# Expert lists of a retrieval layer: one-hot rows used one step later from three buffers, and 32 tiles of values for both token blocks in place of 33

## The chip, the cores and the metric

The kernel runs on one core of a Trainium2 chip. The metric is the device time of one execution in microseconds (us). Before the change three runs took 1665.8, 1665.89 and 1667.91 us, so the median is 1665.89 us.

## The reference, cut to what matters

256 tokens of width 2048 go through one layer: a pooling and an attention branch with an output projection, then a product-key retrieval over 16,384 experts, then a gated embedding. What the change touches is the retrieval:

```python
e1, e2 = ...                     # top 16 of 128 keys, 8 heads, two halves
eidx = e1 * 128 + e2             # 128 experts for each token
gates = softmax(vs)
def block(args):                 # 128 tokens at a time: two blocks
    xb, ib, gb = args
    act = gelu(einsum('tkd,td->tk', expert_u[ib], xb))
    return einsum('tk,tkd->td', act * gb, expert_v[ib])
```

So a row of `expert_v` matters only where `act * gb` is not zero for some token.

## The kernel before, in words

Every float32 product is made of three matmuls of split operands (`mm3`, lines 198 to 200): ScalarE casts a part of a raw tile to the high half (line 91), VectorE subtracts to get the low half (line 93).

After the front, the U stage computes the hidden units of all 128 x 128 experts, one row of 128 experts per step (`feat_mm`, `u_done`), times their gates, into coefficients [expert, token] that SyncE writes to DRAM (`write_coefs`). Free moments between the rows take side tasks: `used` (the largest coefficient of each expert in each block), and then in three stages (rows 0 to 95, 96 to 119, 120 to 127, `STAGES`) the making of lists. `classes` sorts the experts by the blocks that use them: both, the first alone, the second alone. `ranks` and `places` give each used expert a place in the list of its class. The lists have `CAPS` tiles of 128 places. An expert whose rank lies beyond its list is left over, and `places3` notes that in `over`.

`columns` (line 1026) then makes one-hot rows for four rows of experts at a time: `ol` (place within a tile, line 1040), `oh` (tile, line 1041, times the expert's number within its row, line 1042, and times the number of the row, line 1043). `into_list` (line 1048) multiplies them on TensorE, four matmuls per group (line 1053), and `list_end` and `indices` turn the sum into row numbers of V and of the coefficients. A place that no expert took gets row 0 of V and the row of zeros of the coefficients.

The V stage goes tile by tile over the lists (`v_tile`, line 1150): GpSimd gathers 128 rows of V (1 MB, `load_v`, line 1106) and the 128 rows of coefficients (`coef_load`, line 1119); ScalarE and VectorE split both; TensorE makes 24 matmuls of 128x512 for a tile of both blocks, 12 for a tile of one block. V's raw tiles lie in two pools in turn: tile numbers that are odd in `vraw` (three buffers), even ones from number 14 on in `raw` of the weight stream. The first 17 tiles (`EARLY`) are of the first block alone, and 11 of them run between the last rows of U; the others follow in an order that spreads the classes evenly (lines 167 to 175), and the last tile is always the last one for both blocks (`last_tile`). Six tiles before the end the stream takes two `raw` slots for weights (lines 1301 to 1303). From the first projection of the embeddings until tile 17, TensorE, VectorE and ScalarE run in the order of the code; everywhere else a planner orders them. GpSimd's and SyncE's queues run in the order in which their instructions stand.

The gate and the output end the kernel (`tail`, line 1306). Behind it stands a branch (line 1413): when `over` says that an expert found no place, `all_values` (line 1378) computes the sum again over all 128 tiles of V with a loop, one tile per turn, every tile with a single buffer, and the tail runs once more.

Of the kernel before, what the change touches and what calls it, by code (L numbers as in the profile page):

```python
# [19 lines left out]
P = 128  # L20
T = 256
# [8 lines left out]
# tiles of 128 experts that tokens of both blocks use, or of the first or the second block alone  # L30
CAPS = (33, 32, 32)
# [3 lines left out]
# the lists grow in stages, as the rows of 128 experts come; the first tiles of the first block alone  # L35
# start before the last stage
# [3 lines left out]
# of them, those between the last rows' hidden units, from this row on  # L40
BETWEEN = 11
START = 116
# parts of V that Pool splits, while the last lists are made
ON_POOL = (1, 2)
# columns of the lists, for pairs of bf16
# [5 lines left out]
class Feed:  # L51
    """The stream of weights: loads run ahead of the splits, splits ahead of the products."""
# [52 lines left out]
def emit(tc, a):  # L105
# [27 lines left out]
    # ---------------------------------------------------------------- the stream  # L133
# [34 lines left out]
    # tiles for both blocks and for one block in turn, so that loads and products keep pace  # L168
# [11 lines left out]
    # the last units wait for the values  # L180
# [15 lines left out]
    # ---------------------------------------------------------------- helpers  # L196
# [16 lines left out]
    def tok_mm(kts, n, lhs, psl, after=None, t_major=False):  # L213
        """psl[t][:, :n] = sum over kts of lhs[:, kt, t]^T @ W, parts of W from the stream."""
        lh, ll = lhs
        kts = list(kts)
        i = 0
        part = 0
        while i < len(kts):
            wh, wl, w = feed.get()  # L220
            k = w // n
            whv = wh.rearrange("p (k n) -> p k n", n=n)
            wlv = wl.rearrange("p (k n) -> p k n", n=n)
            order = [(j, t) for j in range(k) for t in range(2)]
            if t_major:
                order = [(j, t) for t in range(2) for j in range(k)]
            for j, t in order:
                kt = kts[i + j]
                ts = slice(t * P, (t + 1) * P)
                mm3(psl[t][:, :n], lh[:, kt, ts], ll[:, kt, ts], whv[:, j, :], wlv[:, j, :],  # L230
                    start=(i + j == 0), stop=(i + j == len(kts) - 1))
            i += k
            (after or hook)(*((part,) if after else ()))
            part += 1

    def feat_mm(bh, bl, ps, after):
        """ps[:, :T] = W^T @ (bh + bl), W [P, KT, 128] from the stream."""
        for i in range(2):
            wh, wl, _ = feed.get()
            whv = wh.rearrange("p (k n) -> p k n", n=P)  # L240
            wlv = wl.rearrange("p (k n) -> p k n", n=P)
            for j in range(8):
                kt = 8 * i + j
                mm3(ps[:, :T], whv[:, j, :], wlv[:, j, :], bh[:, kt, :], bl[:, kt, :],
                    start=(kt == 0), stop=(kt == KT - 1))
            if i == 0:
                after(0)

    # ---------------------------------------------------------------- front: loads and constants
# [6 lines left out]
    # the gains come with the first k-tile of x  # L256
# [55 lines left out]
    # ---------------------------------------------------------------- input projection, query latents  # L312
# [3 lines left out]
    def after_q(part):  # L316
        # part 0..3 are the k-tiles of the first unit, then two k-tiles each
        if part in (0, 4, 6):
            g = {0: 1, 4: 2, 6: 3}[part]
            if part == 0:  # L320
                xl[2] = load_x(2)
            split_x(g, xl[g])
            if part == 4:
                xl[3] = load_x(3)
# [3 lines left out]
    # small operands  # L328
# [18 lines left out]
    # latents: statistics and transposes (in the slots of y)  # L347
# [7 lines left out]
    # the latents stay unscaled by the norm of x: it goes into the scale of what follows them  # L355
# [13 lines left out]
    def lat_norm(i):  # L369
        # rstd1 * rsqrt(rstd1^2 * mean(z^2) + eps)  # L370
        for _ in range(2):
            dve.tensor_tensor(ssl[:, :, i], ssl[:, :, i], rstd1, op=OP.mult)
        rsqrt_mean(rl[:, :, i], ssl[:, :, i], 512, f1)
        dve.tensor_tensor(rl[:, :, i], rl[:, :, i], rstd1, op=OP.mult)
# [53 lines left out]
    # ---------------------------------------------------------------- queries, keys and values  # L428
# [88 lines left out]
    # ---------------------------------------------------------------- pool channels  # L517
# [28 lines left out]
    # ---------------------------------------------------------------- attention, pooling, output projection  # L546
# [11 lines left out]
    def scores(j):  # L558
        """two heads: keys of block 0 for the first queries, all keys for the second"""
# [92 lines left out]
    # ---------------------------------------------------------------- h and its norms  # L652
# [5 lines left out]
    # every value twice, side by side  # L658
# [73 lines left out]
    # ---------------------------------------------------------------- retrieval  # L732
# [55 lines left out]
    def slots_T(t):  # L788
        pt = bank()
        for i, s in enumerate((e12[t][:, 0], e12[t][:, 1], gate[t])):  # L790
            pe.transpose(pt[:, i * P:(i + 1) * P], s.rearrange("p h k -> p (h k)"), ident)
        ts = slice(t * P, (t + 1) * P)
        dve.tensor_copy(e1T[:, ts, :], pt[:, 0:P, None].to_broadcast([P, P, 2]))
        dve.tensor_copy(e2T[:, ts, :], pt[:, P:2 * P, None].to_broadcast([P, P, 2]))
        # the gates as a sum of three bf16 values, which is exact
        rest = sel.tile([P, P], F32, name="grest", tag="grest")
        part = sel.tile([P, P], BF16, name="gpart", tag="gpart")
        dve.tensor_copy(rest, pt[:, 2 * P:3 * P])
        for i in range(3):
            dve.tensor_copy(part, rest)  # L800
            if i < 2:
                dve.tensor_copy(gT[:, i, ts, :], part[:, :, None].to_broadcast([P, P, 2]))
                dve.tensor_tensor(rest, rest, part, op=OP.subtract)
            else:
                dve.tensor_copy(gT2[:, ts], part)
# [43 lines left out]
    # ---------------------------------------------------------------- hidden units and gates of all experts  # L849
# [32 lines left out]
    def group(g):  # L882
        """gates of four tokens, by expert; the first tiles hold activations already"""
# [26 lines left out]
    # coefficients to DRAM: a row of zeros, the first N0 rows of 128 experts, the others  # L910
# [16 lines left out]
    def used(lo, hi, b):  # L927
        """the largest coefficient of each expert in a block"""
# [12 lines left out]
    def open_vp():  # L941
# [3 lines left out]
        st["pr"] = vp.tile([P, 2 * T], F32, name="pr")  # L945
# [15 lines left out]
    def classes(s):  # L961
        """experts by the blocks that use them: both, the first alone, the second alone"""
# [18 lines left out]
    def ranks(s):  # L981
        """the place of each expert in the list of its class"""
# [7 lines left out]
    def places(s):  # L990
# [5 lines left out]
        for c in range(3):  # L996
# [3 lines left out]
            if c == 1 and s == len(STAGES) - 2:  # L1000
                dve.scalar_tensor_tensor(ok, r, EARLY * P - 0.5, ok, op0=OP.is_gt, op1=OP.mult)
# [17 lines left out]
    def places3(s):  # L1019
        # experts that found no place  # L1020
# [5 lines left out]
    def columns(s, k):  # L1026
        """the experts i1 = k to k + 3 of all i2: their places, and i1 + 1 and i2 there"""
        if s < 2:
            into_list(s)
# [9 lines left out]
        oh = st["vp"].tile([P, 2, 4, NL], BF16, name="oh", tag="oh", bufs=2)  # L1039
# [8 lines left out]
    def into_list(s):  # L1048
        out = st["list"][:, :2 * NL].rearrange("p (a n) -> p a n", a=2)
        while st["oh"]:  # L1050
# [13 lines left out]
    def indices(i):  # L1064
        """rows of V and of the coefficients; a free place takes any row of V and the zero coefficients"""
# [10 lines left out]
        # rows of half the tokens for the experts of one block  # L1076
# [61 lines left out]
    def last_tile(after):  # L1138
        """the values of the last tile, for both blocks, one after the other"""
# [10 lines left out]
    def v_tile(n, f, after=lambda i: None):  # L1150
        """the values of one tile of experts"""
# [28 lines left out]
    for j in range(NE):  # L1180
        ps = bank()
        if j == 0:
            # the scores of the last keys, then the front's memory is given back
# [22 lines left out]
        # the experts in use so far, from here on with all of their coefficients  # L1206
# [26 lines left out]
    # ---------------------------------------------------------------- per-layer embedding, first half  # L1233
    vp = st["vp"]
    pp = [vp.tile([P, D], F32, name=f"pp{t}") for t in range(2)]
# [4 lines left out]
    def proj(n, between=lambda: None):  # L1240
        """the embeddings' columns; what follows runs while the banks are read"""
# [36 lines left out]
    # ---------------------------------------------------------------- values  # L1278
# [26 lines left out]
    # ---------------------------------------------------------------- gate and output  # L1305
# [71 lines left out]
    # ---------------------------------------------------------------- lists that were too short  # L1377
    def all_values():
        """the sum over all experts, in their order, for inputs that use more than the lists hold"""
# [117 lines left out]
```

## Time and profile before

| what | value |
|---|---|
| median of three runs | 1665.89 us |
| the profiled execution (its span) | 1666.6 us |
| TensorE busy | 1641.0 us, 98% of the span, 11295 matmuls |
| VectorE busy | 1229.6 us, 74% |
| ScalarE busy | 914.9 us, 55% |
| GpSimd busy | 367.4 us, 22% |
| DMA traffic | 354.27 MB, mean 213 GB/s |

The page lists the profiled execution's time as its span, 0.7 us above the median. TensorE is busy nearly all of the time, so what another engine does counts only where TensorE waits for it. The few such waits are found in TensorE's timeline, where the number in brackets behind an instruction is the idle time before it and what ended it.

### The profile page before, as it was taken

Reading aid. Unit: us, or ns where it says so; the run is one execution under the profiler, and the core shown is the slowest. Engines: PE = TensorE matmul, PEld = TensorE weight load, DVE = VectorE, ACT = ScalarE, POOL = GpSimd, SP = SyncE. Lnnn points to the kernel's source line nnn. Section 1 sums busy time; section 2 is a strip of 40 time slices with the busy share of each in tenths; the row PEclk is TensorE's granted clock in tenths of the full one; section 3 lists DMA queues with packets and bytes.
Section 4 is the critical chain, followed back from the end, with each engine's and each line's share of the span. In section 5 each row is a group of like instructions: output and inputs, shape, how many; then the busy total and the mean of one; then the engine's idle time right before and its main releaser. Section 6 shows DMA issues by size and latency. Waiting matters only on the chain.

```text
span 1666.6 us, 29151 instructions
## 1 busy us (share of the span) xinstructions
PE 1641.0 (98%) x11295; PEld 1497.1 (90%) x11295; DVE 1229.6 (74%) x2299; ACT 914.9 (55%) x1598; POOL 367.4 (22%) x355
## 2 busy tenths in 40 slices
PE   8999999999999999999999999999989999999998
PEld 7888788999999999999999999999967888888886
DVE  6575667999986888998765558767786667667764
ACT  7765446544544777776444443345555566566653
POOL 0010000000000333333000000042256677766000
PEclk9999999999999999999999999999999999999999
DMA  8652356445555344444787554578678888888463
GB/s 304 224 194 101 128 201 223 159 176 178 179 182 181 142 151 151 136 151 148 259 277 277 205 203 166 189 291 282 224 271 316 287 298 295 282 298 290 153 219 111
DMA packets 55044, 354.27 MB, mean 213 GB/s; under 512 B 7633, under 2 KB 8786, under 8 KB 14578
## 3 DMA queue, kind: packets, MB, share of 16 engines
q1 hardware_dynamic: 35426, 239.08, 41.2%
q0 software_dynamic: 17600, 110.24, 18.6%
q10 hardware_dynamic: 1872, 3.02, 0.5%
q8 instruction: 90, 1.47, 0.3%
q14 instruction: 56, 0.46, 0.1%
HBM read 331.34 MB, written 20.97 MB: 211 GB/s over the span
## 4 chain that ended last, share of the span: by engine, by line
PE 95%; DVE 2%; DMA 1%; ACT 1%; issue 1%; DVEq 0%; ACTq 0%
PE bank L198 30%; PE bank L199 29%; PE bank L200 29%; PE bank L887 3%; DVE lo L93 1%; DMA raw<-in_w_in_q 1%; PE bank L1053 1%; ACT hi L91 1%; PE bank L815 0%; DMA raw<-in_V,idx 0%; PE bank L570 0%; PE bank L572 0%; PE bank L612 0%; PE bank L1329 0%; PE bank L693 0%
## 5 line engine op out<-in xcount | busy, mean ns | idle before, releaser
L93 DVE TENSOR_TENSOR lo<-raw,hi 128x1024 fp32r<-128x1024 f32 (+2 forms) x498 | 602.3, 1212 | 261.8 <-ACT hi L91 254.5
L91 ACT CAST hi<-raw 128x1024 fp32r<-128x1024 f32 (+2 forms) x498 | 513.9, 1033 | 494.9 <-PE bank L199 333.5
L198 PE MATMUL bank<-xnH,hi 128*128 128x256 f32 x2048 | 589.0, 288 | 0.4 <-issue 0.4
L200 PE MATMUL bank<-xnH,lo 128*128 128x256 f32 x2048 | 581.0, 284 | 0.8 <-DVE lo L93 0.8
L199 PE MATMUL bank<-xnL,hi 128*128 128x256 f32 x2048 | 580.9, 284 | 0.0
L198 PEld LDWEIGHTS bank<-xnH,hi 128*128 128x128 f32 x2048 | 391.9, 191 | 1.4 <-issue 0.6
L200 PEld LDWEIGHTS bank<-xnH,lo 128*128 128x128 f32 x2048 | 391.7, 191 | 1.3 <-DVE lo L93 1.0
L199 PEld LDWEIGHTS bank<-xnL,hi 128*128 128x128 f32 x2048 | 392.0, 191 | 0.4
L1119 POOL DMA_INDIRECT cr<-coefD,idx x97 | 129.3, 1333 | 372.3 <-ACT hi L91 295.0
L199 PE MATMUL bank<-lo,ccH 128*128 128x512 f32 x520 | 205.7, 396 | 1.3 <-issue 0.7
L200 PE MATMUL bank<-hi,ccL 128*128 128x512 f32 x520 | 205.1, 394 | 0.0
L876 POOL TENSOR_TENSOR oo<-m,gT 128x256 bf16<-128x256 bf16 x128 | 86.0, 672 | 423.6 <-DVE oo L874 252.4
L93 DVE TENSOR_TENSOR lo<-vraw,hi 128x1024 fp32r<-128x1024 f32 x108 | 131.4, 1224 | 53.8 <-ACT hi L91 50.7
L198 PE MATMUL bank<-hi,ccH 128*128 128x512 f32 x520 | 155.9, 397 | 2.0 <-ACT hi L91 2.0
L91 ACT CAST hi<-vraw 128x1024 fp32r<-128x1024 f32 x110 | 115.2, 1049 | 64.5 <-PE bank L200 42.7
L199 PEld LDWEIGHTS bank<-lo,ccH 128*128 128x128 f32 x520 | 98.2, 189 | 25.1 <-DVE lo L93 1.4
L198 PEld LDWEIGHTS bank<-hi,ccH 128*128 128x128 f32 x520 | 97.5, 189 | 24.6 <-ACT hi L91 2.9
L200 PEld LDWEIGHTS bank<-hi,ccL 128*128 128x128 f32 x520 | 98.2, 189 | 22.5
L211 ACT ACTIVATE oo<-m,gT 128x128 bf16<-128x128 bf16 x256 | 89.2, 399 | 45.5 <-DVE m L873 39.5
L1106 POOL DMA_INDIRECT vraw<-in_V,idx x55 | 70.7, 1286 | 67.7 <-DVE lo L93 29.2
L198 PE MATMUL bank<-hgH,hi 128*128 128x256 f32 x256 | 72.6, 284 | 1.0 <-ACT hi L91 1.0
L200 PE MATMUL bank<-hgH,lo 128*128 128x256 f32 x256 | 72.9, 287 | 0.0
(319 smaller groups left out, 2283.1 us busy)
## 6 DMA issues: line engine op xcount, KB each, us to landing
raw<-in_U SPq DMA_DIRECT2D x128, 1024.0 KB, 4.9
raw<-in_w_out SPq DMA_DIRECT2D x16, 1024.0 KB, 4.8
raw<-in_w_pq SPq DMA_DIRECT2D x16, 1024.0 KB, 4.8
raw<-in_w_gate SPq DMA_DIRECT2D x16, 1024.0 KB, 4.8
raw<-in_w_in_p SPq DMA_DIRECT2D x8, 1024.0 KB, 4.9
coefD<-CA SPq DMA_DIRECT2D x8, 1024.0 KB, 8.7
coefD<-CB SPq DMA_DIRECT2D x7, 1024.0 KB
raw<-in_w_in_kv SPq DMA_DIRECT2D x8, 576.0 KB, 3.4
```

Of the source, the lines that this page charges most:

```text
L91: self.nc.scalar.copy(hi[:, :w], r)
L93: eng.tensor_tensor(lo[:, :w], r, hi[:, :w].bitcast(F32), op=OP.subtract)
L198: pe.matmul(ps, ah, bh, start=start, stop=False)
L199: pe.matmul(ps, ah, bl, start=False, stop=False)
L200: pe.matmul(ps, al, bh, start=False, stop=stop)
L211: act.activation(dst, ps, AF.Copy, scale=scale)
L876: (pool if k else dve).tensor_tensor(pairs(oo[:, k]), pairs(m1), gT[:, k, tk:tk + 2, None, :].to_broadcast(sh), op=OP.mult)
L887: pe.matmul(pt[:, i * P:(i + 1) * P], o2, o1[k], start=(k == 0), stop=(k == 2))
L1053: pe.matmul(out, ol, oh, start=(k == STAGES[s]), stop=(k == STAGES[s + 1] - 1))
L1106: pool.indirect_dma_start(out=raw, out_offset=None, in_=a["V"], in_offset=bass.IndirectOffsetOnAxis(ap=row(c, i, 0), axis=0))
L1119: pool.indirect_dma_start(out=cr[:, :w], out_offset=None, in_=src, in_offset=bass.IndirectOffsetOnAxis(ap=row(c, i, 1), axis=0))
```

## The change

The list for both blocks gets 32 tiles in place of 33, so the tables `NT` (97 to 96) and `NL` (98 to 96) shrink, and with them the width of the one-hot rows `oh` and of the products on them (196 to 192 columns). `oh` has three buffers in place of two. `columns` multiplies, in the first two stages, all groups but the newest one, before it makes its own, where it multiplied all of them; in the third stage two are kept. The test that the place of an expert of the first block alone lies behind the `EARLY` tiles, done in the last stage only, is now done in the second stage too. The buffers `pp` of the embeddings are allocated earlier, and the embeddings' input `pr` lies in one of them.

```diff
-CAPS = (33, 32, 32)
+CAPS = (32, 32, 32)
...
-        st["pr"] = vp.tile([P, 2 * T], F32, name="pr")
+        st["pp"] = [vp.tile([P, D], F32, name=f"pp{t}") for t in range(2)]
+        st["pr"] = st["pp"][1][:, :2 * T]
...
-            if c == 1 and s == len(STAGES) - 2:
+            if c == 1 and s > 0:
...
     def columns(s, k):
-        if s < 2:
-            into_list(s)
+        into_list(s, 1 if s < 2 else 2)
...
-        oh = st["vp"].tile([P, 2, 4, NL], BF16, name="oh", tag="oh", bufs=2)
+        oh = st["vp"].tile([P, 2, 4, NL], BF16, name="oh", tag="oh", bufs=3)
...
-    def into_list(s):
+    def into_list(s, keep=0):
         out = st["list"][:, :2 * NL].rearrange("p (a n) -> p a n", a=2)
-        while st["oh"]:
+        while len(st["oh"]) > 4 * keep:
...
-    pp = [vp.tile([P, D], F32, name=f"pp{t}") for t in range(2)]
+    pp = st["pp"]
```

On VectorE, at the start of the second stage's one-hot rows (`lf` holds the places, `lo` is the low half of a V or U tile, `CB` the coefficients), before:

```order
L1016 CAST lf<-lhi 128x2x48
L1040 TENSOR_TENSOR ol<-iotab,lf 128x512
L1041 TENSOR_TENSOR oh<-iotab,lf 128x392
L1040 TENSOR_TENSOR ol<-iotab,lf 128x512
L1041 TENSOR_TENSOR oh<-iotab,lf 128x392
L1040 TENSOR_TENSOR ol<-iotab,lf 128x512
L1042 TENSOR_SCALAR oh<-oh,i2col 128x392 x2
L93 TENSOR_TENSOR lo<-raw,hi 128x1024
L907 TENSOR_TENSOR CB<-gl,CB 128x256
L1043 TENSOR_TENSOR oh<-oh,used 128x392 x2
```

And after the change, at the same place:

```order
L1017 CAST lf<-lhi 128x2x48
L1040 TENSOR_TENSOR ol<-iotab,lf 128x512
L1041 TENSOR_TENSOR oh<-iotab,lf 128x384
L1040 TENSOR_TENSOR ol<-iotab,lf 128x512
L1041 TENSOR_TENSOR oh<-iotab,lf 128x384
L1040 TENSOR_TENSOR ol<-iotab,lf 128x512
L1041 TENSOR_TENSOR oh<-iotab,lf 128x384
L1042 TENSOR_SCALAR oh<-oh,i2col 128x384
L93 TENSOR_TENSOR lo<-raw,hi 128x1024
L1042 TENSOR_SCALAR oh<-oh,i2col 128x384
L907 TENSOR_TENSOR CB<-gl,CB 128x256
L1042 TENSOR_SCALAR oh<-oh,i2col 128x384
```

A third `oh` is begun before the first two are finished, so the first row of line 1043, which TensorE waits for, comes one compare and one multiply later.

On GpSimd, the last gathers of V (`vraw`, `raw`, 2048 wide) and of the coefficients (`cr`, 256 wide for both blocks, 128 for one), before:

```order
L1119 DMA cr<-coefD,idx_11063 128x256
L1106 DMA vraw<-in_V,idx_11063 128x2048
L1119 DMA cr<-coefD,idx_11063 128x128
L1119 DMA cr<-coefD,idx_11063 128x256
L1106 DMA raw<-in_V,idx_11063 128x2048
L298 TENSOR_TENSOR rstd_17778<-rs_v,nhalf 128x2
```

And after:

```order
L1120 DMA cr<-coefD,idx_11064 128x256
L1120 DMA cr<-coefD,idx_11064 128x128
L1107 DMA vraw<-in_V,idx_11064 128x2048
L1120 DMA cr<-coefD,idx_11064 128x256
L1107 DMA raw<-in_V,idx_11064 128x2048
L298 TENSOR_TENSOR rstd_17738<-rs_v,nhalf 128x2
```

The queue is one gather of V and one of coefficients shorter. With one tile less the numbers of the last tiles change their parity, and so the pool. The last V gather of the queue before is that of the last tile (number 96, `raw`). After the change the last tile is number 95 and goes to `vraw`; its gather stands ahead of that of tile 94, which is the `raw` one at the queue's end.

## Rows read from the trace of the kernel before

**Rows 1.** The page, busy time of each engine, its share and instructions.
```profile
PE 1641.0 (98%) x11295; PEld 1497.1 (90%) x11295; DVE 1229.6 (74%) x2299; ACT 914.9 (55%) x1598; POOL 367.4 (22%) x355
```
**Rows 2.** Windows: length, PE, PEld, DVE, ACT, POOL busy, clock, DMA share, GB/s.
```profile
1400.00:1500.00 100.00, 100.00 (x432) 81.09 (x431) 67.91 (x76) 59.38 (x77) 69.57 (x53) 1.00 0.84 295
```
**Rows 3.** Timeline of PE: start, duration, instruction, idle before and releaser.
```profile
1012.23 0.50 PE L1053 MATMUL bank<-oh,ol 128*128 128x196 bf16 x4 [0.28 <-DVE oh L1043]
...
1170.26 0.51 PE L1053 MATMUL bank<-oh,ol 128*128 128x196 bf16 x4 [0.64 <-DVE oh L1043]
```
**Rows 4.** Waits of DVE at line 1041: total us, count, longest.
```profile
DVE oh L1041 <- PE bank L1053: 13.4, 18, 0.9
```
**Rows 5.** Timeline of POOL, DVE and PE around the third list.
```profile
1220.37 2.41 POOL L93 TENSOR_TENSOR lo<-vraw,hi 128x1024 fp32r<-128x1024 f32 x1 [6.00 <-DVE cf L1003]
...
1220.62 0.17 DVE L1001 SCALAR_TENSOR_TENSOR ok<-bank,ok 128x8 f32<-128x8 f32 x1
1220.82 1.99 DVE L1002 TENSOR_TENSOR used<-used,ok 128x8 f32<-128x8 f32 x1
...
1223.39 3.04 DVE L1022 TENSOR_TENSOR used<-used 128x8 f32<-128x8 f32 x1
...
1227.93 0.35 DVE L1041 TENSOR_TENSOR oh<-iotab,lf 128x392 bf16<-128x392 bf16 x1
...
1229.09 0.81 PE L1053 MATMUL bank<-oh,ol 128*128 128x196 bf16 x4 [4.81 <-DVE oh L1043]
```
**Rows 6.** Windows after the third list and at the start of the V stage.
```profile
1230.00:1235.00 5.00, 4.55 (x17) 3.59 (x16) 4.76 (x16) 0.98 (x2) 1.87 (x2) 0.68 0.29 113
...
1255.00:1260.00 5.00, 2.96 (x12) 1.81 (x11) 2.52 (x3) 3.45 (x5) 0.37 (x1) 1.00 1.00 399
```
**Rows 7.** Timeline of POOL, SP and PE at the last tile of V.
```profile
1538.59 0.95 POOL L1119 DMA_INDIRECT cr<-coefD,idx  x1 [2.34 <-DVE ccL L208]
...
1544.43 0.33 SPq L76 DMA_DIRECT2D raw<-in_w_gate  x1
...
1552.57 0.94 POOL L1106 DMA_INDIRECT raw<-in_V,idx  x1 [13.04 <-DVE lo L93]
...
1560.36 0.50 PE L199 MATMUL bank<-lo,ccH 128*128 128x512 f32 x1 [0.41 <-DVE lo L93]
```
**Rows 8.** Windows: the first 0.6 us of four gathers of V.
```profile
1205.20:1205.80 0.60, 0.60 (x4) 0.50 (x3) 0.43 (x1) 0.60 (x3) 0.00 (x0) 1.00 1.26 218
1505.00:1505.60 0.60, 0.60 (x4) 0.51 (x3) 0.60 (x2) 0.60 (x2) 0.60 (x1) 1.00 1.33 218
1519.90:1520.50 0.60, 0.60 (x4) 0.49 (x3) 0.60 (x2) 0.49 (x2) 0.60 (x1) 1.00 1.02 218
1554.20:1554.80 0.60, 0.60 (x4) 0.50 (x3) 0.00 (x0) 0.39 (x1) 0.00 (x0) 1.00 1.04 410
```
**Rows 9.** Windows: four gathers of coefficients.
```profile
1503.00:1504.20 1.20, 1.20 (x7) 0.98 (x6) 0.57 (x2) 1.05 (x1) 1.20 (x1) 1.00 0.42 171
1522.70:1523.70 1.00, 1.00 (x6) 0.83 (x5) 0.37 (x2) 0.92 (x1) 1.00 (x1) 1.00 0.40 94
1534.40:1535.50 1.10, 1.10 (x6) 0.89 (x6) 0.00 (x0) 0.61 (x1) 0.80 (x2) 1.00 0.44 175
1541.10:1542.20 1.10, 1.10 (x7) 0.88 (x6) 1.10 (x3) 0.30 (x2) 0.00 (x0) 1.00 0.25 82
```
**Rows 10.** The page: groups at lines 93 and 91, and the loads of U.
```profile
L93 DVE TENSOR_TENSOR lo<-raw,hi 128x1024 fp32r<-128x1024 f32 (+2 forms) x498 | 602.3, 1212 | 261.8 <-ACT hi L91 254.5
L91 ACT CAST hi<-raw 128x1024 fp32r<-128x1024 f32 (+2 forms) x498 | 513.9, 1033 | 494.9 <-PE bank L199 333.5
...
raw<-in_U SPq DMA_DIRECT2D x128, 1024.0 KB, 4.9
```
**Rows 11.** Timeline of PE after a wait, and SP's last instruction.
```profile
1232.39 0.63 PE L198 MATMUL bank<-hi,ccH 128*128 128x512 f32 x1
1232.82 0.58 PE L199 MATMUL bank<-lo,ccH 128*128 128x512 f32 x1
...
1661.94 0.34 SPq L1362 DMA_DIRECT2D out_h<-o  x1
```

## The prediction, made before the changed kernel was run

> **What bounds the kernel now.** I read the busy times first: TensorE works 98% of the span [rows 1], and a window in the V stage shows it with no idle time, 432 matmuls in 100 us at full clock [rows 2]. So only two things can make the kernel faster: fewer matmuls, or the removal of one of TensorE's few waits. The timeline of TensorE gives those near the change: 0.28 and 0.64 us at the first list products of the first two stages [rows 3], 4.81 us at the third list [rows 5], about 2 us early in the V stage (2.96 us busy in a window of 5) [rows 6], and 0.41 us at the last tile of V [rows 7]. The profiled span is 1666.6 us, 0.7 above the median; I sum against the span and take 0.7 off at the end.
>
> **The change part by part.** The tile for both blocks is the large term. It has 24 matmuls of 128x512, and one takes 100 / 432 = 0.2315 us [rows 2]: -5.56 us. Its two gathers and its splits go too, but lie beside TensorE's work.
>
> The last V gather. GpSimd waits 13.04 us before it issues it, because weights took `raw` slots (the last at 1544.43), and TensorE waits 0.41 us for the split of that tile [rows 7]. Afterwards the last tile lies in `vraw`, with a free slot, and the gather that stands behind the weights is tile 94's, released by the split of tile 92, a tile of one block whose parts are split sooner before TensorE needs them. I take -0.4. Bounds: -0.4 (the wait is gone) and +0.5 (tile 94 is as late as tile 96 was, and as much again).
>
> One-hot rows one step later. VectorE waits 13.4 us in 18 places for TensorE to release an `oh` [rows 4]. With three buffers these waits go, but nothing that TensorE waits for stands behind them apart from the starts of the stages, so they are worth 0. At these starts VectorE now makes one compare more (0.35 us) and about one multiply of like size, and in the second stage the new test (0.17, the row of the third stage) before the first product is released [rows 5]. TensorE has two V matmuls more in front of it, 0.46 us. So 0.87 - 0.46 = +0.4. Bounds: -0.9 (both waits of [rows 3] vanish) and +1.0 (both stages pay the whole 0.5 or so).
>
> In the first stage the list is read after eight products in place of four; four take 0.50 us [rows 3], and indices and first gathers wait for them. Bounds 0 and +0.5; I take +0.1, since V tiles are not yet due then.
>
> The 128 list products shrink by 4 of 196 columns. By 0.50 us for four [rows 3] that is at most 128 x 0.125 x 4 / 196 = -0.33; a part of each is not columns, so -0.2.
>
> The third list's wait of 4.81 us stays. It is made by two tiny VectorE instructions of 1.99 and 3.04 us that run while GpSimd splits a part of V in 2.41 us [rows 5], and the order there is that of the code, untouched.
>
> The order of the tiles from number 17 changes from 0, 1, 2, 0, 2 (0 = both blocks) to 0, 1, 2, 2, 0. Tile 20 holds half the work, while V still comes at 399 GB/s with all DMA time taken [rows 6]. I take 0, as the work only comes a tile later; the bound is one half tile, 12 x 0.2315 = +2.8, less the wait that is there anyway.
>
> Sum: -5.56 - 0.4 + 0.4 + 0.1 - 0.2 = -5.7, a span of 1660.9, and so 1660.2 us by the median.
>
> **Do the lists still hold?** This decides more than all else. If more than 32 x 128 = 4096 experts are used by both blocks, `over` is set and `all_values` runs. The trace shows two marks of the free places, which all read one and the same row. A gather of full tiles starts slowly: 218 GB/s at a DMA share of 1.26 (173 for a full share) and 218 at 1.33 (164). The last tile of the first block alone, of whose places about a fifth are taken (31.2 tiles, counted from the reference's inputs), starts with 218 at 1.02 (214). The 33rd tile for both blocks starts with 410 at 1.04: 394 [rows 8], more than twice a full tile's rate. Its coefficient gather, issued at 1538.59 [rows 7], is slow in turn: 82 at 0.25 is 328, like that of the nearly free tile (94 at 0.40: 235), whereas a full tile has 171 at 0.42 (407) and the 32nd tile for both blocks 175 at 0.44 (398) [rows 9]. So the 32nd tile is full or within a few places of it, and the 33rd is free or nearly so. I take it that the 33rd holds nothing. A handful of experts there I can't exclude by these marks.
>
> What makes the number uncertain is where ScalarE's gelu is exactly zero. Counted from the reference's inputs: 31.4 tiles if it is zero below -7, 31.95 below -7.4, 32.08 below -7.5, 32.8 below -8. [...]
>
> **The rivals.** First, the fallback. A few experts of the 33rd tile would set `over`, and the loop runs 128 times with one buffer of each kind. [...] The turn's end lies between 0 and the 4.7 us from SyncE's last issue to the end of the span (1666.6 - 1661.94) [rows 11]. Low: 4.9 + 2.2 + 5.6 = 12.7; high: 4.9 + 4.5 + 10.3 + 4.7 = 24.4. The middle is 18.5, times 128 is 2370, and a second tail of about 1666.6 - 1560.4 = 106 [rows 7] comes on top: 1660 + 2370 + 106, about 4140 us (3400 to 4900). For it: the list is within a few places of its end. Against it: the 33rd tile's gather starts like no gather of different rows.
>
> Second, the lists hold, but V is late: tile 20 gives back its half tile, 2.8 us, and the last gather is as late as before (0.4). Then -5.7 + 2.8 + 0.4 = -2.5: 1663.4. For it: the DMA share of 1.00 and TensorE's 2 us of waiting in that window [rows 6]; against: the transfers there run ahead of the casts of ScalarE, busy 3.45 us of 5.
>
> Third, the change does not do what it says on VectorE: the third buffer is bought by the delay at both starts, and the planner's other order in the U stage costs as much as the row at 1170.26, 0.64 us, twice more. This gives 1660.2 + 1.3 = 1661.5 and is within the likeliest case's range.
>
> **How the numbers follow.** The forecast with its bounds has a chance of 0.68, the late V of 0.10, the fallback of 0.20, and 0.02 is left for something else that costs time. The forecast's own range is 1658 to 1663. To leave out no more than 2 in 10, the range is 1657.5 to 1666: it holds the late V, and not the fallback. This kernel can tell about 0.2%, 3.3 us, from no change. Faster by more than that: nearly all of the forecast, 0.67. Within it: the late V and the edge of the forecast, 0.11. Slower: the fallback and the rest, 0.22.
>
> **What would show it.** Right: a span near 1661, 432 matmuls per 100 us in the V stage, 24 fewer in all, no wait of 0.41 us at the last tile, no VectorE waits at line 1041, and the coefficient gather of the last tile as fast as a full one. The fallback would show 128 x 24 = 3072 matmuls more, some 134 MB of V more, and a low share of TensorE. The late V would show in the window of 1255 to 1260 as more than 2 us idle. Wrong would be a TensorE with the same number of waits and a span above 1664.

## The result and the profile after

The changed kernel takes 1652.24 us in the median of three runs (1651.8 to 1653.38), against 1665.89 before: a ratio of 0.9917 (0.9899 to 0.9934), 13.65 us less. The forecast said 1660.2 and had the direction and the first term right, but less than half of the size, and the time lies below its range.

The lists hold: no matmul of the fallback is in the trace. The page's busy times of the changed kernel answer to [rows 1]:

```profile
span 1651.7 us, 29081 instructions
...
PE 1626.3 (98%) x11271; PEld 1490.9 (90%) x11271; DVE 1226.1 (74%) x2297; ACT 912.5 (55%) x1595; POOL 359.1 (22%) x353
```

24 matmuls fewer, as expected, but TensorE is busy 14.7 us less, and 24 matmuls are worth 5.6. Most of the rest is in the pace, the time from the start of one matmul to the start of the next. The windows of the changed kernel that answer to [rows 2] and to the second row of [rows 6] (length, busy time and count of PE, PEld, DVE, ACT, POOL, then clock, DMA share, GB/s):

```profile
1400.00:1500.00 100.00, 100.00 (x443) 82.84 (x442) 70.82 (x80) 62.84 (x80) 70.99 (x54) 1.00 0.85 303
1255.00:1260.00 5.00, 5.00 (x24) 4.13 (x23) 4.75 (x5) 3.98 (x5) 3.81 (x4) 1.00 1.03 410
```

443 matmuls where there were 432, without idle time in either, at the same granted clock of 1.00. The second window has lost its 2 us of idle time: the feared late V is not there. TensorE's timeline shows the pace, here over seven differences from start to start, first in the V stage before the change (1.63 us), then after it (1.59):

```profile
1300.22 0.39 PE L199 MATMUL bank<-lo,ccH 128*128 128x512 f32 x1
...
1301.85 0.39 PE L200 MATMUL bank<-hi,ccL 128*128 128x512 f32 x1
```

```profile
1299.97 0.39 PE L199 MATMUL bank<-lo,ccH 128*128 128x512 f32 x1
...
1301.56 0.39 PE L200 MATMUL bank<-hi,ccL 128*128 128x512 f32 x1
```

In the trace, whose starts are finer than these lines, successive starts lie 0.226 to 0.227 us apart after the change, in 1398 of 1497 cases. Before the change the differences run 0.232, 0.231, 0.232, 0.228, 0.230, 0.233, 0.241 in a circle, to within 0.001, with a mean of 0.2324 over 1520 of them (353.3 us; after: 340.1 us for 1497, 0.2272). The products of the gate at the kernel's end, of the same shape, have 0.2269 before and 0.2268 after, and the U stage's products together take 724.5 us before and 724.6 after. So only the V stage became quicker, by 2.2% for each matmul. The gate in the kernel before has 134 matmuls in 30 us, where its V stage has 131:

```profile
1600.00:1630.00 30.00, 30.00 (x134) 24.86 (x133) 17.15 (x17) 13.04 (x14) 0.00 (x0) 1.00 0.69 234
```

TensorE's waits in the changed kernel, the answer to [rows 3] and the last line of [rows 5]:

```profile
1012.46 0.49 PE L1054 MATMUL bank<-oh,ol 128*128 128x192 bf16 x4 [0.76 <-DVE oh L1043]
...
1170.81 0.73 PE L198 MATMUL bank<-hi,ccH 128*128 128x512 f32 x2 [1.13 <-ACT hi L91]
...
1229.72 0.80 PE L1054 MATMUL bank<-oh,ol 128*128 128x192 bf16 x4 [4.81 <-DVE oh L1043]
```

Both starts of stages cost about half a microsecond more (0.28 to 0.76, 0.64 to 1.13), the third list's wait is the same to the hundredth. VectorE's waits for TensorE have moved rather than gone, as its waits show (total us, count, longest; compare [rows 4]):

```profile
DVE ol L1040 <- PE bank L1054: 14.2, 22, 0.8
```

With three `oh` it now waits at `ol`, which shares a ring of three buffers with other small tiles. At the end the last tile's V gather (`vraw`) is issued 10 us ahead of the queue's last one (`raw`, of tile 94), and TensorE does not wait for the last tile (0.41 in [rows 7]):

```profile
1523.17 0.94 POOL L1107 DMA_INDIRECT vraw<-in_V,idx  x1 [2.72 <-DVE lo L93]
...
1533.50 0.94 POOL L1107 DMA_INDIRECT raw<-in_V,idx  x1 [7.30 <-DVE lo L93]
```

### The profile page after: what moved, and what is told of

Same layout as the page of the kernel before. It is cut to its first block, busy times and chain, and to the rows that moved or that the text cites. A ratio compares the mean times of both kernels' runs of the same rounds, so it can differ in the third digit from the quotient of the medians.

```text
span 1651.7 us, 29081 instructions
## 1 busy us (share of the span) xinstructions
PE 1626.3 (98%) x11271; PEld 1490.9 (90%) x11271; DVE 1226.1 (74%) x2297; ACT 912.5 (55%) x1595; POOL 359.1 (22%) x353
## 3 DMA queue, kind: packets, MB, share of 16 engines
q0 software_dynamic: 17408, 109.06, 18.5%
## 4 chain that ended last, share of the span: by engine, by line
PE 96%; DVE 1%; DMA 1%; ACT 1%; issue 0%; DVEq 0%; ACTq 0%
PE bank L198 30%; PE bank L199 30%; PE bank L200 30%; PE bank L887 3%; PE bank L1054 1%; DMA raw<-in_w_in_q 1%; ACT hi L91 1%; DMA cr<-coefD,idx 1%; DVE lo L93 0%; PE bank L815 0%; PE bank L570 0%; PE bank L572 0%; PE bank L612 0%; PE bank L1330 0%; PE bank L693 0%
## 5 line engine op out<-in xcount | busy, mean ns | idle before, releaser
L1120 POOL DMA_INDIRECT cr<-coefD,idx x96 | 125.2, 1304 | 366.9 <-ACT hi L91 295.3
L199 PE MATMUL bank<-lo,ccH 128*128 128x512 f32 x512 | 200.4, 391 | 0.6 <-DVE lo L93 0.6
L200 PE MATMUL bank<-hi,ccL 128*128 128x512 f32 x512 | 199.7, 390 | 0.0
L198 PE MATMUL bank<-hi,ccH 128*128 128x512 f32 x512 | 149.4, 391 | 1.1 <-ACT hi L91 1.1
```

The source lines that it names most:

```text
L198: pe.matmul(ps, ah, bh, start=start, stop=False)
L199: pe.matmul(ps, ah, bl, start=False, stop=False)
L200: pe.matmul(ps, al, bh, start=False, stop=stop)
L1120: pool.indirect_dma_start(out=cr[:, :w], out_offset=None, in_=src, in_offset=bass.IndirectOffsetOnAxis(ap=row(c, i, 1), axis=0))
```

## The experiments

The clue was that the pace changed for the products of `ccH` and `ccL` and for no others. In the memory of a partition, as the build places the tiles, `hi` begins at byte 27,584 and `lo` at 39,872 in both kernels; `ccH` begins at 123,456 before and at 139,200 after. Modulo 256 these are 192, 192, 64 and 192: in the V stage the stationary operands (`ccH`, `ccL`: the trace of the kernel before has a weight load of 128x128 for each of their matmuls, with a median of 188 ns) were 128 bytes out of step with the moving ones (`hi`, `lo`: 128x512 for each matmul), and the change, by moving `pp` ahead, adding an `oh` and narrowing the tables, happened to put them in step. Below, "distance" is the start of the one operand minus that of the other, modulo 256; the pace is the mean difference of successive matmul starts in the trace, longer ones than 0.3 us left out.

**128 bytes in the kernel before.**

```diff
         st["vp"] = vp
+        vp.tile([P, 32], F32, name="pad")
```

> The kernel before, with an unused tile of 128 bytes per partition at the start of the pool that holds the V stage's tiles: the split coefficients ccH and ccL, the stationary operands of the V stage, start at 192 instead of 64 bytes past a multiple of 256, as they do after the change; nothing else differs. Theory A (the start address of these operands, in steps of 128 bytes, sets the pace of the V stage's matmuls): 0.2267 us between matmuls instead of 0.2323, over some 1570 of them, so about 8.5 us less, 1657.4 us. Theory B (the change put these tiles some 16 KB elsewhere, into another part of the memory, and 128 bytes are nothing): 1665.9 us, 0.2323. Theory C (third buffer, one step later, narrower one-hot rows made the matmuls faster): 1665.9 us, 0.2323.

Measured: 1658.44 us, ratio to before 0.9945 (0.9929 to 0.9962), pace 0.2270. Its window in the V stage:

```profile
1400.00:1500.00 100.00, 100.00 (x443) 82.81 (x442) 70.22 (x79) 60.98 (x79) 69.64 (x52) 1.00 0.85 297
```

The same 443 as in the changed kernel, by 128 unused bytes. Theory A holds; B and C fall. `ccH` now begins 375 times 256 bytes behind `hi`, in the changed kernel 436 times: an odd and an even multiple are both quick, and half a multiple more or less is slow, which is why the distances here are taken modulo 256.

**128 bytes in the changed kernel**, the same edit.

> The changed kernel with the same unused 128 bytes: ccH and ccL start at 64 past a multiple of 256, as before the change. Theory A: the V stage's matmuls go back to 0.2323 us apart, about 8.5 us more, 1660.7 us, which is what the prediction gave. Theories B and C: 1652.2 us, 0.2267.

Measured: 1661.57 us, ratio to before 0.9962 (0.9949 to 0.9974), pace 0.2324.

```profile
1400.00:1500.00 100.00, 100.00 (x432) 81.09 (x431) 69.50 (x78) 60.51 (x77) 70.89 (x53) 1.00 0.83 290
```

432 as in [rows 2]. By its ratio this is 6.3 us below before, with the forecast's 5.7 inside the interval: without the address effect the forecast's sum comes out. That it does so this closely is in part luck: in this trace TensorE's waits from 980 us on are 1.9 us shorter in sum than before (8.8 in place of 10.7), where the forecast had them 0.1 longer, and the stretch behind TensorE's last matmul is 0.5 longer. The two ratios multiply to 0.9907, beside the change's own 0.9917, which is inside the intervals.

**The moving operands moved instead.**

```diff
+            if self.pad is None:
+                self.pad = self.pool.tile([P, 32], F32, name="pad", tag="pad", bufs=1)
             hi = self.pool.tile([P, 1024], F32R, name="hi", tag="hi")
```

> The kernel before with the unused 128 bytes in the stream's pool, ahead of the moving operands hi and lo: hi, lo and all that lies behind them move from 192 to 64 past 256 (the gate's stationary gH too), ccH and ccL from 64 to 192. Theory A1 (what counts is the distance of stationary from moving operand, 128 bytes modulo 256 being the slow one): the V stage stays at 0.2323 us, the gate at 0.2267, about 1666 us. Theory A2 (what counts is the stationary operand's own start, 64 being the slow one): the V stage goes to 0.2267, the gate's 384 matmuls to 0.232, 1666 - 8.5 + 2 = 1659.5 us. Theories B and C: no change.

Measured: one run, 1670.99 us; V stage 0.2332, gate 0.2268. The gate's operands all start at 64 here and are quick; `ccH` starts at 192 and is slow, since `hi` is at 64. So it is the distance (A1), not a start of its own. The time is 2.6 us above that of the kernel before in the same series (1668.43). The trace has it in the V stage's matmuls, 2.8 us longer in sum than before: 1.3 by the pace (0.2332 for 0.2324), and most of the rest behind TensorE's waits at 1257 us, where the granted clock is 0.80 and 0.86 in two windows of 5 us and was 1.00 before.

**Only the V stage's operands moved**: the 128 bytes just ahead of `ccH`.

> The kernel before with the unused 128 bytes just ahead of ccH: ccH, ccL and the embeddings' tiles move to 192 past 256, while the gathered rows (vraw, cr) and the one-hot rows stay where they are. Theory A for the stationary operands: as with the 128 bytes at the pool's start, 0.2267 us and about 1657.4 us. If it is the address of the gathered rows or of the one-hot rows that counts: 0.2323 us and 1665.9 us.

Measured: one run, 1658.8 us, pace 0.2271. The gathered rows and the one-hot rows have no part in it.

**The list edits alone.**

```diff
-CAPS = (32, 32, 32)
+CAPS = (33, 32, 32)
...
         st["vp"] = vp
+        vp.tile([P, 24], F32, name="pad")
```

> The changed kernel with 33 tiles for both blocks again (CAPS 33), and 96 unused bytes at the start of the V stage's pool so that ccH and ccL keep their distance of 0 modulo 256 from hi and lo: what is left of the change are the list edits alone (one step later, three buffers, the test in the second stage). If these are worth nothing, as the prediction's +0.4 - 0.9 = -0.5 or so says, it takes what the kernel before takes at that distance, 1658.4 us, and stands 5.6 to 6 above the changed kernel's 1652.2. If the list edits carried part of the gain, it lies below 1657.

Measured: 1658.91 us, ratio 0.9949 (0.9932 to 0.9965), where the kernel before at the same distance has 0.9945. The list edits are worth nothing that shows. The changed kernel's 0.9917 against 0.9949 is then the tile: 5.3 us of 1665.89 (by the two intervals, give or take 4), where the forecast had 5.56 and 0.4 for the last gather.

**Other distances in the V stage**: 32 and 64 unused bytes in place of 128.

> The changed kernel with 32 unused bytes: the stationary operands' distance from the moving ones is 32 modulo 256. If only a distance near 128 is slow, the V stage stays at 0.2267 us and 1652 us. If any distance but 0 costs, it lies between 0.2267 and 0.2323, up to 1661 us. If some distance is quicker than 0, below 0.2267.

> The same with 64 unused bytes, a distance of 64 modulo 256. Only near 128 slow: 0.2267 us, 1652 us. A cost that grows with the distance: about 0.2295, 1656 us. As at 128: 0.2323, 1661 us.

Measured, one run each: 1660.94 us and 0.2333; 1660.15 us and 0.2334. So 128 is nothing special: 32 and 64 cost as much. "Only near 128" and "grows with the distance" both fall.

**lo alone, and all that lies behind it, by 64.**

```diff
+            if self.pad is None:
+                self.pad = self.pool.tile([P, 16], F32, name="pad", tag="pad", bufs=1)
             lo = self.pool.tile([P, 1024], F32R, name="lo", tag="lo")
```

> The changed kernel with 64 unused bytes between hi and lo in the stream's pool: lo and all that lies behind it, ccH, ccL and the gate's and the U stage's operands too, move by 64, hi stays. In the V stage and in the gate two of three matmuls then have a moving operand (hi) at a distance of 64 from the stationary one, the third (lo) at 0; in the U stage, where hi and lo are stationary, two of three likewise. Theory M1 (each matmul pays for its own distance): V stage and gate at 0.2267 + two thirds of 0.0065 = 0.231 us. Theory M2 (one operand out of step spoils the run of matmuls): 0.233 us. If the short matmuls of 256 columns pay as well (6144 in the U stage), 0.12 us becomes more, and the kernel 10 to 40 us slower than 1652; if only the long ones do, about 1652 + 7 + 2 = 1661 us.

Measured: one run, 1653.1 us. The V stage took 0.2302 and the gate 0.2325 (M1 said 0.231, M2 0.233 for both: the one stage is near M1, the other nearer M2, so neither is right as put). What I had not expected is the U stage: its matmuls of 256 columns became quicker, 713.5 us for 5930 of them in place of 724.6 in the changed kernel. That called for the next three.

**Everything but the weight stream with its hi and lo moved**, by 32, 64 and 128 (the edit for 64):

```diff
     s2_cm, s2 = open_pool(name="s2")
+    s2.tile([P, 16], F32, name="pad")
```

> The changed kernel with 64 unused bytes behind lo: everything but the weight stream moves by 64, so that all products of split weights have stationary and moving operand 64 apart modulo 256. The matmuls of 512 columns should take 0.2333 us as with 64 bytes in the V stage alone, some 900 more of them than the V stage's, +16 us. The U stage: in the run with lo alone moved its matmuls of 256 columns became quicker, 713.5 instead of 724.5 us for 5930 of them, where two of three had a distance of 64. Theory D1 (the short ones gain by the distance, each its own share): 724.5 - 16.5 = 708 us, and the whole stays near 1652. Theory D2 (they gained because hi and lo differ in start): no gain, 724.5, whole 1668.

> The same with 32 bytes. D1: the U stage gains about as at 64, 708 us, long matmuls 0.2333. D2: 724.5 and 1668.

> The same with 128 bytes. D1: the U stage gains, perhaps by another amount, long matmuls 0.232. D2: 724.5 and 1666.

Measured, one run each; the rows give the distance, the pace of the V stage, the pace of the gate, the sum of the U stage's differences (5930 of them, 5931 at 128), and the time:

| distance | V stage | gate | U stage | time |
|---|---|---|---|---|
| 0 (changed kernel) | 0.2272 us | 0.2268 us | 724.6 us | 1652.24 us |
| 32 | 0.2334 | 0.2333 | 709.6 | 1653.96 |
| 64 | 0.2334 | 0.2333 | 705.3 | 1647.14 |
| 128 | 0.2324 | 0.2324 | 719.1 | 1659.63 |

D1 holds: the long matmuls lose at any distance tried but 0, the short ones gain, most at 64 (D1 had 708). The whole at 64 is 5 us quicker than D1's 1652: by the traces all long matmuls cost 17 us (D1 had 16), and besides the U stage's 19.3 some 3 us come from the other products of 256 columns and from shorter waits. The window of 600 to 700 us shows it in the U stage, first the changed kernel, then the one at 64:

```profile
600.00:700.00 100.00, 100.00 (x972) 97.88 (x971) 89.66 (x217) 73.29 (x207) 34.08 (x50) 1.00 0.42 147
```

```profile
600.00:700.00 100.00, 100.00 (x985) 97.93 (x984) 90.53 (x220) 73.34 (x207) 34.39 (x50) 1.00 0.44 152
```

**GpSimd's two splits given to VectorE.**

```diff
-ON_POOL = (1, 2)
+ON_POOL = ()
```

> The changed kernel with the two splits that GpSimd makes while the third list is built given to VectorE (ON_POOL empty). Theory: the two tiny VectorE instructions of 1.99 and 3.04 us in that stretch are slow because GpSimd splits at the same time; without it they take 0.17 us, 4.7 us less on the path to the third list, against one split of 1.21 us more on VectorE ahead of it: TensorE's wait of 4.8 us becomes about 1.3, and 3 to 4 us are won, 1648.5 us. Rival: they are slow for another reason (a wait not shown), and the two splits come on top: 1652.2 + 2.4 = 1654.6 us.

Measured: 1650.31 us, ratio to before 0.9899 (0.9882 to 0.9915). The two tiny instructions of [rows 5] take 0.17 us each now:

```profile
1220.94 0.17 DVE L1003 TENSOR_TENSOR used<-used,ok 128x8 f32<-128x8 f32 x1
...
1221.70 0.17 DVE L1023 TENSOR_TENSOR used<-used 128x8 f32<-128x8 f32 x1
```

So GpSimd's split made them slow, as said: in [rows 5] the first of them ends at 1222.81 us, and the split beside it at 1222.78. But only some 2 us are won, not 3 to 4, since TensorE now waits for the splits themselves:

```profile
1226.93 0.49 PE L1054 MATMUL bank<-oh,ol 128*128 128x192 bf16 x4 [0.86 <-DVE oh L1043]
...
1233.01 0.50 PE L199 MATMUL bank<-lo,ccH 128*128 128x512 f32 x1 [1.69 <-DVE lo L93]
```

With two more, of 1.09 and 0.58 us, its waits there are 4.2 us in sum, in place of 4.81 and 0.55. In the window of 1230 to 1235 us the granted clock is 0.57 in the changed kernel and 1.00 here. Four list products take 0.49 us in place of 0.80.

**One of the two given to VectorE**: `ON_POOL = (2,)`.

> The changed kernel with only the first of GpSimd's two splits given to VectorE (ON_POOL = (2,)). In the run with both given, 1650.3 us, VectorE's two splits stand in a row after the third list, and TensorE waits 1.69 us for the second. Theory: with the second on GpSimd, starting later, the tiny instructions are over before it and stay quick, and that wait shrinks: about 1649 us. Rival: GpSimd's split runs beside VectorE's one-hot rows or list instructions and slows those instead: 1651 to 1653 us.

Measured: 1653.04 us, ratio 0.991 (0.9891 to 0.993); its profiled run was the longest of four, 1656.66. The rival holds: the split on GpSimd now runs beside the one-hot rows, and a compare that takes 0.43 us in the kernel before takes 2.60:

```profile
1225.27 2.60 DVE L1040 TENSOR_TENSOR ol<-iotab,lf 128x512 bf16<-128x512 bf16 x1
```

**31 tiles for both blocks**: `CAPS = (31, 32, 32)`.

> The changed kernel with 31 tiles for both blocks: asks how full the list of 32 is, and what the fallback costs. By the reading of the gathers (32nd tile full, 33rd free) more than 31 tiles are needed, so over is set, and the loop over 128 tiles and a second tail follow: 1645 + 2370 + 106 = 4120 us (3400 to 4900). Rival: 31 tiles hold, the marks in the gathers meant something else: 1646.5 us.

Measured: one run, 3916.2 us. More than 31 tiles are needed, at most 32. The loop's tiles in the trace, with durations in ns (smallest, median, largest) and the first and last start:

```profile
L198 PE MATMUL bank<-fvh,fch x1024: 387/628/796, 1654.5 to 3798.1; 128*128 128x512 f32 x171
...
L200 PE MATMUL bank<-fvh,fcl x1024: 387/389/398, 1661.0 to 3802.9; 128*128 128x512 f32 x171
```

From 1654.5 to 3802.9 these are 128 turns of 16.8 us, where the forecast had 18.5 between 12.7 and 24.4.

**A version with each stage at its own distance**: both splits on VectorE, and in the U stage 64 bytes between `xnH`, `xnL` and `hi`, `lo`, everywhere else 0. The slots of `xnH` and `xnL` are shared with the gate's `gH` and `gL`, so each stage takes its own slice of a slightly longer slot (the low halves are cut likewise, and three small tiles are packed closer to make room):

```diff
-    xnH = s2.tile([P, KT, T], F32R, name="xnH", tag="yH")
+    xnH = s2.tile([P, KT * T + 16], F32R, name="xnH", tag="yH")[:, 16:16 + KT * T].rearrange("p (k t) -> p k t", t=T)
...
-        gH = s2.tile([P, KT, T], F32R, name="gH", tag="yH")
+        gH = s2.tile([P, KT * T + 16], F32R, name="gH", tag="yH")[:, 0:0 + KT * T].rearrange("p (k t) -> p k t", t=T)
```

> A version meant to beat both: the changed kernel with both early splits on VectorE (1650.3 us by itself), and with the U stage's moving operands xnH and xnL at a distance of 64 bytes modulo 256 from hi and lo, while ccH, ccL, the gate's gH and gL and the front's operands stay at 0 (three small tiles are packed closer to make room). Theory: each matmul pays for its own distance, 256 columns best at 64, 512 columns at 0: 724.5 - 705.3 = 19.2 us less in the U stage, nothing else changed, 1631 us. Rival: the gain of the U stage with all operands moved came from the neighbours' positions or is eaten by the slower of the other engines, since the stream of U then has less time: 1640 us or more.

Measured: 1630.56 us (1629.74 to 1631.22), ratio to before 0.9788 (0.9772 to 0.9805). It beats both kernels: 21.7 us below the changed one, and 19.8 below the run with the splits alone (18.5 by the two ratios). The theory had 1631, its rival 1640 or more. The trace puts the gain where the edit is: the U stage's differences sum to 704.9 us in place of 724.6, while the V stage has 0.2271 and the gate 0.2268, as before the edit. The page of this run:

```profile
span 1628.3 us, 29081 instructions
...
PE 1604.6 (99%) x11271; PEld 1469.3 (90%) x11271; DVE 1223.5 (75%) x2299; ACT 911.5 (56%) x1595; POOL 353.9 (22%) x351
```

## Why the prediction was wrong, point by point

**What bounds the kernel.** Right: TensorE, and nearly all of the gain is time of TensorE. The step that failed stands in that part: "only two things can make the kernel faster: fewer matmuls, or the removal of one of TensorE's few waits". There was a third, the pace of the matmuls themselves. The prediction priced the removed matmuls at 0.2315 us, the average of a window (whose count takes in matmuls that only reach into it; the starts give 0.2324), and did not ask why the same shape took 0.2269 in the gate of the same trace. The change's edits to buffers were read for waits only; that they move every later tile in memory was left out of the sum. The missed term is the V stage's 353.3 us at 0.2324, of which (0.2324 - 0.2272) x 1520 = 7.9 us went.

**The tile.** Right: -5.56 forecast; 5.3 measured by ratios with the last gather included, and the span's sum fits too: -5.6 for the tile, -7.9 for the pace and -1.5 for TensorE's waits (10.7 us in all from 980 us on before, 9.2 after) make -15.0 against a measured -14.9. This close a fit is in part luck: the sum leaves out the list products, which took 0.2 less as forecast (10.1 to 9.9 us), and the stretch from TensorE's last matmul to the end of the span, which grew from 6.9 to 7.9.

**The last gather.** Right: the 0.41 us are gone. With 33 tiles the wait stays whatever the pace (0.76 us in before_pad128, 0.47 in after_33_tiles); with 32 no trace has it.

**One-hot rows one step later.** The direction was right, the size low: +0.4 forecast, +0.97 measured (0.76 + 1.13 - 0.28 - 0.64), just under the upper bound of 1.0. At the second start it was not the one-hot row but a cast of a part of V on ScalarE that ended TensorE's wait. The cast was not late, it starts at 1169.71 us, and at 1169.66 before. But it is what the two V matmuls need that now stand ahead of the list products: the 0.46 us of cover in the forecast were themselves a wait. That VectorE's waits are worth nothing was right, and that they go was not: they moved to `ol`, 14.2 us in place of 13.4. The third rival, that the change does not do on VectorE what it says, came nearest on this point.

**The first lists, the third list.** The gap around 1099 us grew by 0.2, near the +0.1 taken. The third list's wait is 4.81 us in both, as said.

**Tile 20.** I took 0, with a bound of +2.8. The 2 us of idle time in that window [rows 6] went instead. The traces separate order and pace only in part. With the old order and the slow pace the waits at 1257 us are there (2.0 us, and 2.3 in before_hi128); with the old order and the quick pace there are none (before_pad128, before_pad128_cc), nor with the new order and the slow pace in after_pad32 and after_pad64 (0.5 in after_pad128). So in these runs either change was enough to lose them, yet with the new order they are back in after_lo64, 2.0 us. What decides is open.

**Do the lists hold?** The reading of the gathers was right, and tight: 32 tiles hold, 31 do not. The 33rd tile was free, as the quick start [rows 8] said. The chance of 0.2 for the fallback did no harm to the forecast. By the prediction's counts these two runs bound where the gelu becomes exactly zero: if only below -7.5, 32.08 tiles would be needed, and 32 hold; if already below -7, 31.4, and since 31 are too few, the point can't lie far above -7. The price of the fallback, 4140, was 6% too high against the 3916 of 31 tiles. In its two bounds for a turn, 4.9 us is the load of 1 MB [rows 10], 5.6 and 10.3 us are 24 matmuls at 0.2315 and at the 0.43 between two starts soon after a wait [rows 11], where the granted clock is 0.50 (window of 1232 to 1233 us), and 2.2 and 4.5 are one and two pairs of a cast of 1.033 and a subtraction of 1.21 [rows 10]. These are estimates that no run shows as they stand: in the loop of after_31_tiles a turn has one cast of 1.90 us and one subtraction of 2.29, and in two windows of 100 us TensorE is busy 48 and 51 us, at a granted clock of 0.70.

## What to carry to other kernels

When the same matmul shape runs at two paces in one trace (0.2324 us in one stage, 0.2269 in another, both without idle time and at the same clock), ask where its operands lie in memory before pricing it, and difference the starts, since the busy share shows nothing (100 of 100 us at either pace). A change that adds, removes or resizes a buffer moves the tiles behind it, as here, so its effect on stages that it does not touch has to be separated by an unused tile that puts them back. Padding is a cheap experiment: 128 bytes were worth more here (9.2 us by the ratio of 0.9945) than the tile of work that the change removed (5.3).

## What the runs showed of the hardware that I had not expected

- Float32r matmuls of 512 columns with 128x128 weights, back to back: 0.2267 us apart once settled where stationary and moving operand start at the same place modulo 256 bytes, 0.2324 to 0.2334 at distances of 32, 64 and 128. After a wait, the quick case first shows up to nine irregular intervals (0.224 to 0.239) and then settles at 0.226 and 0.227. The slow cases settle too, each on its own pattern: a circle of seven differences from 0.228 to 0.241 at 128, one of six from 0.231 to 0.235 at 32, and 0.233 and 0.234 at 64.
- Matmuls of 256 columns the other way round: 724.6 us for 5930 at distance 0, 709.6 at 32, 705.3 at 64, 719.1 at 128.
- By which mechanism is open, and distances other than 0, 32, 64 and 128 were not tried.
- VectorE's small instructions beside a split on GpSimd: 1.99 and 3.04 us for a tile of 128x8 that takes 0.17 without it, and 2.60 for a compare of 0.43. Each of the three ended within 0.3 us of the end of a split on GpSimd.
